# Half-chunk weight buffers, and two weight sums of the value products added on chip

## The chip, the cores and the metric

The kernel runs on one core of a Trainium2 chip. The metric is the device time of one execution, in microseconds (us). Before the change the median of three runs is 1919.06 us (1919.06 to 1919.16).

The engines go by the names of the profile: PE does matmuls (PEld is its weight load), DVE is VectorE, ACT is ScalarE, POOL is GpSimd, and SP only issues DMA transfers. Each engine runs its own instructions strictly in order, and waits for the others by semaphores.

## The reference

Two layers, each with one wide input projection, three groups of attention heads, a gate, an output projection and a layer norm:

```python
def hybrid_layer(x, mem, w_in, b_forget, w_mem_kv, w_out, ln_gain, ln_bias):
    ...
    h = jnp.einsum('bsd,dn->bsn', x, w_in)
    ...
    y_fox = fox_attention(heads(fq, H_FOX), heads(fk, H_FOX), heads(fv, H_FOX), cum_logf)
    y_fox = y_fox.reshape(b, s, D_FOX) * jax.nn.silu(fg)
    ...
    y_dsa = dsa_attention(...)
    y_mem = memory_attention(heads(mq, H_MEM), k_mem..., v_mem...)
    y = jnp.concatenate([y_fox, y_dsa, y_mem], axis=-1)
    y = jnp.einsum('bsn,nd->bsd', y, w_out)
    return layer_norm(ALPHA * x + y, ln_gain, ln_bias)
```

The sequence has 512 rows, the model 2048 columns, and everything is float32. The change touches only one piece of `x @ w_in`: the columns that make the heads' values, their gates and the first queries and keys, called "values" here.

## The kernel before, in words

**Chunks and halves.** All weights come as chunks of 128x2048 float32 (1 MB), in one long list that sets the order of the program (the main loop at L1051). `load_w` (L234) has SP load a chunk into one of three buffers `raw` (8 KB per partition). A chunk is used in two halves of 1024 columns. `split_w` (L256) splits a half into a high and a low part: ACT writes `whi` (L213), DVE writes `wlo = raw - whi` (L214), into a pool of four pairs. PE then does three matmuls per product, whi by the high part of the left side (L220), wlo by the same (L221), whi by its low part (L222). A half of a value chunk is 12 such matmuls of 512 columns, a chunk 24.

**The order around the change.** Nothing is scheduled by a planner: the main loop writes each engine's instructions in program order. When it stands at half n of chunk i, it first issues `grow_w(i)` and `load_w(i + 2)`, then `split_w(n + 3)`, then PE's matmuls of half n. Between these, `tick` steps generators that make everything else: sums of x for the left sides (`val_operands`, vx, vxh and vxl), the search for the top keys, the stores of values, and `all_sums`.

**Seven products in place of eight.** The value matrix is multiplied as 2x2 blocks with seven products per pair of columns, four pairs to a layer. A product is named (P1, P7, P2, Q6, Q4, Q5, Q3), and each uses either a plain block of weights or a sum of blocks: P7 uses T3 (two blocks), Q6 uses T2, Q4 uses T4, Q5 uses T1 (two blocks). Each has two chunks, g0 and g1. A layer first does P1 P1 P7 P7 P2 Q6 Q6 P2 Q4 Q4 for the four pairs (`VAL_FIRST`), and then Q5 Q5 Q3 Q3 for the four pairs (`VAL_SECOND`), 56 chunks in all. Results are gathered by DVE in `vraw` and added up in DRAM by accumulating stores of POOL.

**Where the sums come from.** T3 and T1 are summed in DRAM by POOL (`weight_sums`, L360): a copy of one block (L377), then an accumulating transfer of the other (L358). Outside the values stage each step is preceded by a tiny `mark` of DVE and `seen` of POOL (`pool_waits`), which hold POOL's queue to DVE's place in the program. SP loads the finished sum like a chunk. T2 and T4 are grown in place: once P7's raw chunk has been split, `grow_w` (L245) has POOL add one block to it in SBUF by an accumulating transfer, which gives Q6's chunk, and one more gives Q4's.

**The next x.** At the end of the first layer `next_x` (L933) normalises 16 tiles z and transposes them into 16 pairs of high and low parts, the odd low parts on POOL (L950), and then stores the 16 tiles to DRAM from POOL's queue (L956).

Of the kernel before, what the change touches and what calls it, by code (L numbers as in the profile page):

```python
# [11 lines left out]
F32 = mybir.dt.float32  # L12
# [74 lines left out]
VAL_OPENS = ("P1", "P7", "P2", "Q5")  # L87
VAL_ENDS = ("P1", "Q4", "P2", "Q3")
GROWN = {"Q6": ("P7", (0, 0)), "Q4": ("Q6", (1, 0))}


def layer_chunks(l):
# [27 lines left out]
def stream():  # L120

    wall = all_chunks()
    where = {c: i for i, c in enumerate(wall)}
    out = []

    def product(kind, l, name, pair, gs=(0, 1)):
        right = PRODUCTS[name][2]
        for g in gs:
            if kind == "val" and name in GROWN:
                of, step = GROWN[name]  # L130
                src = ("grown", (of, where[kind, l, 2 * pair + step[1], 2 * step[0] + g]))
            elif isinstance(right, str):
                src = ("sum", (kind, l, right, pair, g))
            else:
                src = ("wall", where[kind, l, 2 * pair + right[1], 2 * right[0] + g])
            out.append(({"val": "vs"}.get(kind, kind), l, (name, pair), g, src))

    for i, c in enumerate(wall):
        kind, l, j = c[:3]
        if kind == "out":  # L140
            if c == ("out", l, 0, 0):
                for name, pair in OUT_ORDER:
                    product("out", l, name, pair)
        elif kind == "val":
            if c == ("val", l, 0, 0):
                for order in (VAL_FIRST, VAL_SECOND):
                    for pair in range(PAIRS):
# [25 lines left out]
def kernel(  # L173
# [12 lines left out]
):  # L186
    nc = tc.nc
    consts = ctx.enter_context(tc.tile_pool(name="consts", bufs=1))
    raws = ctx.enter_context(tc.tile_pool(name="raws", bufs=3))
    whl = ctx.enter_context(tc.tile_pool(name="whl", bufs=4))  # L190
    slots = ctx.enter_context(tc.tile_pool(name="slots", bufs=71))
    tiny = ctx.enter_context(tc.tile_pool(name="tiny", bufs=3))
# [6 lines left out]
    def uid(name):  # L199
        count[0] += 1  # L200
        return f"{name}_{count[0]}"
# [23 lines left out]
    chunks = stream()  # L225
    raw, parts = {}, {}
    sums = {}
    grows = {}
    place = {c[:4]: i for i, c in enumerate(chunks)}
    for i, (kind, l, j, g, (how, key)) in enumerate(chunks):  # L230
        if how == "grown":
            grows[place[kind, l, (key[0], j[1]), g]] = i

    def load_w(i, pieces=1):  # L234
        if i < len(chunks) and chunks[i][4][0] != "grown":
            raw[i] = raws.tile([P, DM], F32, tag="raw", name=uid("raw"))
            w = DM // pieces
            kind, key = chunks[i][4]
            src = wall[key] if kind == "wall" else sums[key]
            for c in range(pieces):  # L240
                nc.sync.dma_start(raw[i][:, c * w:(c + 1) * w], src[:, c * w:(c + 1) * w])
                if i < 3 and c * 2 % pieces == 0:
                    load_mem(2 * i + c * 2 // pieces)

    def grow_w(i):  # L245

        if i in grows:
            n = grows[i]
            nc.gpsimd.dma_start(raw[n], wall[chunks[n][4][1][1]], accum_op=ALU.add,
                                max_dma_last_dim=4 * DM)  # L250

    def last_half(i):

# [2 lines left out]
    def split_w(n, pieces=1, between=None):  # L256
        i, h = divmod(n, 2)
        if i < len(chunks):
            if last_half(i) and n < 2 * len(chunks) - 3:
                parts[n] = []  # L260
                for c in range(2):
                    hi, lo = slot("wh", F32R), slot("wl", F32R)
                    split(raw[i][:, h * 1024 + c * 512:h * 1024 + (c + 1) * 512], hi, lo)
                    parts[n].append((hi, lo))
                return
            hi = whl.tile([P, DM // 2], F32R, tag="whi", name=uid("whi"))
            lo = whl.tile([P, DM // 2], F32R, tag="wlo", name=uid("wlo"))
            w = DM // 2 // pieces
            for c in range(pieces):
                r = slice(c * w, (c + 1) * w)  # L270
                split(raw[i][:, h * 1024 + c * w:h * 1024 + (c + 1) * w], hi[:, r], lo[:, r])
                if between and c == 0:
                    between()
            parts[n] = (hi, lo)
            if last_half(i):
                parts[n] = [(hi[:, c:c + 512], lo[:, c:c + 512]) for c in (0, 512)]
            if h:
                t = raw.pop(i)
                if i in grows:
                    raw[grows[i]] = t  # L280


    mem_raw = {}

# [104 lines left out]
    def all_sums():  # L389


        for l in range(DEPTH):
            yield from paced(weight_sums("val", l, ("T3", "T1"), range(PAIRS)))
            while now != (l, "heads"):
                yield 1
            yield from paced(weight_sums("out", l, ("T3", "T1", "T2", "T4"), range(2)))
# [382 lines left out]
    def val_operands():  # L779
        add, sub = ALU.add, ALU.subtract  # L780
        a11, a12, a21, a22 = (0, 0), (0, 1), (1, 0), (1, 1)

        for i in range(4):
            val_sum("S3", i, ((a11, 0, add), (a21, 0, sub), (a11, 1, add), (a21, 1, sub)))
            yield 1
        for i in range(4):
            val_hi("S3", i)
            val_sum("S2", i, (("S3", 0, add), (a22, 0, add), (a22, 1, add)))
            yield 1
            val_lo("S3", i)  # L790
            yield 1
        for i in range(4):
            hi, lo = vleft["S2", i] = slot("vxh", F32R), slot("vxl", F32R)
            nc.scalar.activation(hi, vx["S2", i], AF.Copy, scale=-1.0)
            yield 1
            nc.vector.scalar_tensor_tensor(lo, vx["S2", i], -1.0, hi.bitcast(F32),
                                           op0=ALU.mult, op1=ALU.subtract)
        yield from wait_for("P7")
        making.append("S1")
        for n in range(9):  # L800
            if n < 4:
                val_sum("S1", n, ((a11, 0, add), ("S2", 0, sub), (a11, 1, add)))
# [12 lines left out]
        making.clear()  # L815
# [116 lines left out]

    def next_x():  # L933

        ms = [norm_stats(st) for st in range(4)]
        for c in range(4):
            for st in range(4):
                normalise(st, c, *ms[st])
            yield 1
        for k in range(KT):  # L940
            c, o = divmod(k, 4)
            tp = bank("xt")
            for st in range(4):
                nc.tensor.transpose(tp[:, st * P:(st + 1) * P], z[st, c][:, o * P:(o + 1) * P], ident)
            xf, hi, lo = slot("xf"), slot("xh", F32R), slot("xl", F32R)
            nc.scalar.activation(xf, tp, AF.Identity, bias=gcol[:, 1, k:k + 1],
                                 scale=gcol[:, 0, k:k + 1])
            nc.scalar.activation(hi, xf, AF.Copy)
            eng = nc.gpsimd if k % 2 else nc.vector
            eng.tensor_tensor(lo, xf, hi.bitcast(F32), op=ALU.subtract)  # L950
            xT[k] = (hi, lo)
            if k % 2:
                yield 1
        for c in range(4):
            for st in range(4):
                nc.gpsimd.dma_start(x1_d[st * P:(st + 1) * P, c * 512:(c + 1) * 512], z.pop((st, c)))  # L956
                if st % 2:
                    yield 1

    def residual_rows(l):  # L960

# [89 lines left out]
    for i, (kind, l, j, col, _) in enumerate(chunks):  # L1051
# [27 lines left out]
            ps = bank("c")  # L1079
        for h in range(2):  # L1080
            n = 2 * i + h
            if h == 0 and i > 0:
                grow_w(i)
                load_w(i + 2)
                if 2 <= i < 6:
                    for k in range(4 * i - 8, 4 * i - 4):
                        load_xt(k)
                elif i == 7:
                    load_tables()
            if n < 6:  # L1090
                split_mem(n + 2)
            split_w(n + 3)
# [267 lines left out]
```

## Time and profile before

| what | us |
|---|---|
| median of three runs | 1919.06 |
| the profiled execution | 1918.99 |
| its span in the profile | 1916.8 |
| PE busy | 1900.9 |
| DVE busy | 1389.3 |
| ACT busy | 969.6 |
| POOL busy | 355.8 |

The profile shows one execution. Times in it count from the start of the span. A row of a group or of a timeline reads: line, engine, operation, output<-input, shape; behind it are the busy time and what ended the idle time before it. A row of waits reads: who waited for whom, us in total, times, the longest. The values of layer 0 run from 249 to 557 us (the pairs of Q5 and Q3 from 469), those of layer 1 from 1200 to 1508 (Q5 and Q3 from 1420).

### The profile page before, as it was taken

To read this page: it belongs to the slowest core of one execution; us is meant where nothing else is said; L and a number is where in the kernel's file an instruction comes from. 1 tells how busy PE (TensorE), PEld (TensorE's weight loads), DVE (VectorE), ACT (ScalarE), POOL (GpSimd) and SP (SyncE) were. 2 spreads that over 40 slices of the span, in tenths; PEclk is the share of its full clock that TensorE was granted. 3 is DMA by queue.
4 is the path that set the end of the run, shared out by engine and by line. 5 is a ranking of instruction groups with operands and counts; after the bars stand their busy time and mean duration, and the time that the engine had idled before them with its cause. 6 is when DMAs were issued, how large, how long until landed. Compare 5 with 4: busy or idle time off the path is not lost.

```text
span 1916.8 us, 25327 instructions
## 1 busy us (share of the span) xinstructions
PE 1900.9 (99%) x9282; PEld 1620.7 (85%) x9282; DVE 1389.3 (72%) x2343; ACT 969.6 (51%) x1538; POOL 355.8 (19%) x615
## 2 busy tenths in 40 slices
PE   9999999999999999999999999999999999999997
PEld 8998888888888888888899988888888888888886
DVE  6666657779665677688776777667786666677898
ACT  5565454445444455555475644544454444555552
POOL 0231101111123012110052212111111321112101
PEclk9999999999999999999999999999999999999999
DMA  9699888888988778898778989988889888789856
GB/s 365 230 296 323 213 194 235 241 234 239 263 257 233 245 236 240 250 333 310 247 234 269 283 272 258 238 220 236 244 244 261 261 227 244 240 234 268 342 197 154
DMA packets 110712, 484.57 MB, mean 253 GB/s; under 512 B 11504, under 2 KB 44272, under 8 KB 69500
## 3 DMA queue, kind: packets, MB, share of 16 engines
q0 software_dynamic: 32864, 216.05, 45.6%
q1 hardware_dynamic: 77724, 266.90, 38.8%
q8 instruction: 73, 1.20, 0.3%
q14 instruction: 51, 0.42, 0.1%
HBM read 445.14 MB, written 174.09 MB: 323 GB/s over the span
## 4 chain that ended last, share of the span: by engine, by line
PE 93%; DVE 4%; ACT 2%; issue 1%; DMA 0%; SPq 0%; POOL 0%; DVEq 0%; ACTq 0%; POOLq 0%
PE c L220 12%; PE c L222 12%; PE c L221 12%; PE v L222 11%; PE v L220 11%; PE v L221 11%; PE z L221 4%; PE z L222 4%; PE z L220 4%; PE pt L682 1%; PE ix L600 1%; PE ix L599 1%; PE po L222 1%; PE po L221 1%; PE po L220 1%
## 5 line engine op out<-in xcount | busy, mean ns | idle before, releaser
L214 DVE TENSOR_TENSOR wlo<-raw,whi 128x1024 fp32r<-128x1024 f32 (+1 forms) x497 | 607.0, 1225 | 283.5 <-ACT whi L213 281.3
L213 ACT ACTIVATE whi<-raw 128x1024 fp32r<-128x1024 f32 (+1 forms) x497 | 521.9, 1054 | 381.5 <-PE v L222 243.1
L220 PE MATMUL c<-xh,whi 128*128 128x512 f32 (+1 forms) x1056 | 402.1, 381 | 0.0
L222 PE MATMUL c<-xh,wlo 128*128 128x512 f32 (+1 forms) x1056 | 398.3, 377 | 0.0
L221 PE MATMUL c<-xl,whi 128*128 128x512 f32 (+1 forms) x1056 | 397.3, 376 | 0.0
L222 PEld LDWEIGHTS c<-xh,wlo 128*128 128x128 f32 x1056 | 198.2, 188 | 32.4
L221 PEld LDWEIGHTS c<-xl,whi 128*128 128x128 f32 x1056 | 198.5, 188 | 30.5
L220 PEld LDWEIGHTS c<-xh,whi 128*128 128x128 f32 x1056 | 198.3, 188 | 30.0
L220 PE MATMUL v<-whi,vxh 128*128 128x512 f32 x512 | 199.8, 390 | 0.0
L222 PE MATMUL v<-whi,vxl 128*128 128x512 f32 x512 | 199.3, 389 | 0.0
L221 PE MATMUL v<-wlo,vxh 128*128 128x512 f32 x512 | 199.2, 389 | 0.0
L349 POOL TENSOR_TENSOR seen<-mark,mhalf 128x1 f32<-128x1 f32 x128 | 35.3, 276 | 762.2 <-DVE mark L348 727.3
L221 PE MATMUL z<-wlo,yh 128*128 128x512 f32 (+1 forms) x434 | 168.1, 387 | 2.5 <-DVE wlo L214 2.5
L220 PE MATMUL z<-whi,yh 128*128 128x512 f32 (+1 forms) x434 | 168.4, 388 | 0.0
L222 PE MATMUL z<-whi,yl 128*128 128x512 f32 (+1 forms) x434 | 167.8, 387 | 0.0
L220 PE MATMUL v<-whi,xh 128*128 128x512 f32 x384 | 149.4, 389 | 0.0
L221 PE MATMUL v<-wlo,xh 128*128 128x512 f32 x384 | 149.4, 389 | 0.0
L222 PE MATMUL v<-whi,xl 128*128 128x512 f32 x384 | 149.4, 389 | 0.0
L222 PEld LDWEIGHTS v<-whi,vxl 128*128 128x128 f32 x512 | 96.1, 188 | 20.0
L221 PEld LDWEIGHTS v<-wlo,vxh 128*128 128x128 f32 x512 | 96.1, 188 | 19.9
L220 PEld LDWEIGHTS v<-whi,vxh 128*128 128x128 f32 x512 | 96.1, 188 | 19.6
L221 PEld LDWEIGHTS z<-wlo,yh 128*128 128x128 f32 x434 | 81.5, 188 | 20.0 <-DVE wlo L214 4.2
(220 smaller groups left out, 3031.0 us busy)
## 6 DMA issues: line engine op xcount, KB each, us to landing
raw<-in_wall_dram SPq DMA_DIRECT2D x151, 1024.0 KB, 7.2
sum<-in_wall_dram POOLq DMA_DIRECT2D x64, 1024.0 KB, 11.5
raw<-sum SPq DMA_DIRECT2D x64, 1024.0 KB, 7.1
raw<-in_wall_dram POOLq DMA_DIRECT2D x32, 1024.0 KB, 8.1
v<-vraw POOLq DMA_DIRECT2D x96, 256.0 KB, 4.2
vraw<-v SPq DMA_DIRECT2D x64, 256.0 KB, 6.9
x<-z POOLq DMA_DIRECT2D x32, 256.0 KB, 8.1
memraw<-in_memt_dram SPq DMA_DIRECT2D x16, 256.0 KB, 7.3
```

The costliest lines, as they stand in the source:

```text
L213: nc.scalar.activation(hi, src, AF.Copy)
L214: nc.vector.tensor_tensor(lo, src, hi.bitcast(F32), op=ALU.subtract)
L220: nc.tensor.matmul(ps, ah, bh, start=start, stop=False, skip_group_check=more)
L221: nc.tensor.matmul(ps, ah, bl, start=False, stop=False, skip_group_check=more)
L222: nc.tensor.matmul(ps, al, bh, start=False, stop=stop, skip_group_check=more)
L349: nc.gpsimd.tensor_tensor(seen, mark, mhalf, op=ALU.mult)
L599: nc.tensor.matmul(o, st[:, qb * P:(qb + 1) * P], kh2[:, :w], start=True, stop=False)
L600: nc.tensor.matmul(o, st[:, qb * P:(qb + 1) * P], kl2[:, :w], start=False, stop=True)
L682: nc.tensor.transpose(tp[tb][:, toff + (qb - kt) * P:toff + (qb - kt + 1) * P], pr[b][:, off + kt * P:off + (kt + 1) * P], ident)
```

## The change

**Buffers.** `raw` becomes six buffers of half a chunk in place of three of a whole one, in the same space. A chunk is loaded in two transfers of 512 KB, and each half comes free by itself.

**T4 on DVE.** Q4's sum is no longer grown by a transfer. T4 is T2 plus a block, and that block is the one that P2 has just used. `make_w` adds P2's raw half to Q6's in place, behind the split of whichever comes later in the program. T2 is still grown by POOL, by halves.

**T1 on DVE.** The chunk of Q5 is no longer loaded as a finished sum. SP loads one block into the raw half and the other into two small slots `other` (128x512), and `pair_w(n + 4)` adds them, one half earlier than `split_w(n + 3)`. `weight_sums` for the values makes T3 alone.

**Two smaller edits.** `val_operands` waits six steps before the splits of S2 (`yield 6`), and `next_x` stores column c - 1 while it makes column c.

```diff
-    raws = ctx.enter_context(tc.tile_pool(name="raws", bufs=3))
+    raws = ctx.enter_context(tc.tile_pool(name="raws", bufs=6))
...
+            elif kind == "val" and right in PAIRED:
+                src = ("pair", tuple(at(step) for step in PAIRED[right]))
...
+            if j[0] == "Q6":
+                grows[of] = i
+            else:
+                lender = place[kind, l, ("P2", j[1]), g]
+                makes[max(of, lender)] = i
+                lends[i] = (of, lender)
...
+                if c * 2 % pieces == 0:
+                    raw[i].append(raws.tile([P, H], F32, tag="raw", name=uid("raw")))
+                nc.sync.dma_start(raw[i][-1][:, c * w % H:c * w % H + w], src[:, c * w:(c + 1) * w])
...
+                if kind == "pair":
+                    for e in (2 * c, 2 * c + 1):
+                        t = slot("other")
+                        nc.sync.dma_start(t, wall[key[1]][:, e * 512:(e + 1) * 512])
+                        others[i, e] = t
...
+    def pair_w(n):
+
+        i, h = divmod(n, 2)
+        if i < len(chunks) and chunks[i][4][0] == "pair":
+            for e in range(2):
+                d = raw[i][h][:, e * 512:(e + 1) * 512]
+                nc.vector.tensor_tensor(d, d, others.pop((i, 2 * h + e)), op=ALU.add)
...
+    def make_w(i, h):
+
+        to = makes[i]
+        of, lender = lends[to]
+        t = raw.setdefault(to, [None, None])[h] = raw[of][h]
+        nc.vector.tensor_tensor(t, t, raw[lender][h], op=ALU.add)
+        raw[of][h] = raw[lender][h] = None
...
+            if i in makes:
+                make_w(i, h)
...
-            yield from paced(weight_sums("val", l, ("T3", "T1"), range(PAIRS)))
+            yield from paced(weight_sums("val", l, ("T3",), range(PAIRS)))
...
+        yield 6
         for i in range(4):
             hi, lo = vleft["S2", i] = slot("vxh", F32R), slot("vxl", F32R)
...
+                for st in (o - 1, o) if c else ():
+                    store(st, c - 1)
                 yield 1
...
+            grow_w(n + 2)
             if h == 0 and i > 0:
-                grow_w(i)
                 load_w(i + 2)
...
+            pair_w(n + 4)
             if n < 6:
                 split_mem(n + 2)
             split_w(n + 3)
```

How this moves instructions is shown at three places of layer 0. The first is DVE's order where the first Q5 chunks are prepared. In the kernel before, the halves of pair 0's two Q5 chunks give the wlo rows numbered 4253, 4275, 4295 and 4321. Here is the piece from the second to the last of these:

```order
L214 TENSOR_TENSOR wlo_4275<-raw_4228,whi_4274 128x1024
L777 TENSOR_TENSOR vxl_4250<-vx_2310,vxh_4249 128x512
L214 TENSOR_TENSOR wlo_4295<-raw_4272,whi_4294 128x1024
L859 TENSOR_TENSOR vraw_3954<-vraw_3954,v_3961 128x512
L859 TENSOR_TENSOR vraw_3956<-vraw_3956,v_3962 128x512
L767 TENSOR_TENSOR vx_2531<-xh_678,vx_2531 128x256
L767 TENSOR_TENSOR vx_2531<-vx_2531,xl_679 128x256
L767 TENSOR_TENSOR vx_2531<-xh_682,vx_2531 128x256
L767 TENSOR_TENSOR vx_2531<-vx_2531,xl_683 128x256
L214 TENSOR_TENSOR wlo_4321<-raw_4272,whi_4320 128x1024
```

In the changed kernel the same four halves are the wlo rows 4290, 4324, 4346 and 4374 (L218). L275 is `pair_w`. What is left out are the sums of x, the vxl and two adds of results, as before:

```order
L275 TENSOR_TENSOR raw_4251<-raw_4251,other_4253 128x512
L275 TENSOR_TENSOR raw_4251<-raw_4251,other_4255 128x512
...
L275 TENSOR_TENSOR raw_4257<-raw_4257,other_4259 128x512
L275 TENSOR_TENSOR raw_4257<-raw_4257,other_4261 128x512
L218 TENSOR_TENSOR wlo_4290<-raw_4251,whi_4289 128x1024
...
L275 TENSOR_TENSOR raw_4309<-raw_4309,other_4311 128x512
L275 TENSOR_TENSOR raw_4309<-raw_4309,other_4313 128x512
L218 TENSOR_TENSOR wlo_4324<-raw_4257,whi_4323 128x1024
...
L275 TENSOR_TENSOR raw_4315<-raw_4315,other_4317 128x512
L275 TENSOR_TENSOR raw_4315<-raw_4315,other_4319 128x512
L218 TENSOR_TENSOR wlo_4346<-raw_4309,whi_4345 128x1024
...
L218 TENSOR_TENSOR wlo_4374<-raw_4315,whi_4373 128x1024
```

Eight adds of 128x512 stand ahead of the last of the four, two for each half. Each pair of adds comes one half before the wlo that reads it.

The second place is DVE's order a little earlier, at the last P2 and Q6 chunks. Before:

```order
L214 TENSOR_TENSOR wlo_4092<-raw_3920,whi_4091 128x1024
L777 TENSOR_TENSOR vxl_4065<-vx_4041,vxh_4064 128x512
L214 TENSOR_TENSOR wlo_4112<-raw_4089,whi_4111 128x1024
...
L214 TENSOR_TENSOR wlo_4134<-raw_4089,whi_4133 128x1024
L777 TENSOR_TENSOR vxl_4109<-vx_4083,vxh_4108 128x512
L214 TENSOR_TENSOR wlo_4154<-raw_3881,whi_4153 128x1024
```

and in the changed kernel, where L293 is `make_w`:

```order
L218 TENSOR_TENSOR wlo_4114<-raw_3936,whi_4113 128x1024
L823 TENSOR_TENSOR vxl_4086<-vx_4061,vxh_4085 128x512
L218 TENSOR_TENSOR wlo_4134<-raw_4109,whi_4133 128x1024
L293 TENSOR_TENSOR raw_3934<-raw_3934,raw_4109 128x1024
...
L218 TENSOR_TENSOR wlo_4156<-raw_4111,whi_4155 128x1024
L293 TENSOR_TENSOR raw_3936<-raw_3936,raw_4111 128x1024
L823 TENSOR_TENSOR vxl_4131<-vx_4104,vxh_4130 128x512
L218 TENSOR_TENSOR wlo_4177<-raw_3892,whi_4176 128x1024
```

Two adds of 128x1024 have come in here, behind the wlo of the two halves of P2's g1. Two more stand behind the halves of Q6's g0, four and three wlo rows earlier than the first of these. All four stand ahead of the rows of the first place.

The third place is SP's queue. Before, a chunk is one row, and pair 0's Q5 chunks are loaded from the finished sums:

```order
L241 DMA raw_3964<-in_wall_dram 128x2048
L241 DMA raw_4089<-in_wall_dram 128x2048
L241 DMA raw_4228<-sum_1605 128x2048
L241 DMA raw_4272<-sum_1660 128x2048
L241 DMA raw_4318<-in_wall_dram 128x2048
```

In the changed kernel the same chunk of P2 and the first of Q5:

```order
L258 DMA raw_4109<-in_wall_dram 128x1024
L258 DMA raw_4111<-in_wall_dram 128x1024
L258 DMA raw_4251<-in_wall_dram 128x1024
L264 DMA other_4253<-in_wall_dram 128x512
L264 DMA other_4255<-in_wall_dram 128x512
L258 DMA raw_4257<-in_wall_dram 128x1024
L264 DMA other_4259<-in_wall_dram 128x512
L264 DMA other_4261<-in_wall_dram 128x512
```

A Q5 chunk is six transfers in place of one, and twice the bytes. PE's order is the same in both kernels; POOL loses 16 copies, 16 accumulating steps and the marks of these (T1, over both layers), and 16 transfers that grew Q4.

More of the change, by code (lines that the diff above doesn't have):

```diff
@@ L89 @@
 GROWN = {"Q6": ("P7", (0, 0)), "Q4": ("Q6", (1, 0))}
+PAIRED = {"T1": ((0, 0), (0, 1))}
 def layer_chunks(l):
@@ L128, in product @@
         for g in gs:
+            at = lambda step: where[kind, l, 2 * pair + step[1], 2 * step[0] + g]
             if kind == "val" and name in GROWN:
                 of, step = GROWN[name]
-                src = ("grown", (of, where[kind, l, 2 * pair + step[1], 2 * step[0] + g]))
+                src = ("grown", (of, at(step)))
+            elif kind == "val" and right in PAIRED:
+                src = ("pair", tuple(at(step) for step in PAIRED[right]))
             elif isinstance(right, str):
@@ L134, in product @@
             else:
-                src = ("wall", where[kind, l, 2 * pair + right[1], 2 * right[0] + g])
+                src = ("wall", at(right))
             out.append(({"val": "vs"}.get(kind, kind), l, (name, pair), g, src))
@@ L227 @@
     sums = {}
-    grows = {}
+    grows, makes, lends = {}, {}, {}
     place = {c[:4]: i for i, c in enumerate(chunks)}
@@ L231, with half, load_w @@
         if how == "grown":
-            grows[place[kind, l, (key[0], j[1]), g]] = i
-    def load_w(i, pieces=1):
+            of = place[kind, l, (key[0], j[1]), g]
+            if j[0] == "Q6":
[4 more added lines that the diff above has]
+                lends[i] = (of, lender)
+    H = DM // 2
+    def half(src, h):
+        return src[:, h * H:(h + 1) * H]
+    def load_w(i, pieces=2):
@@ L235, in load_w @@
         if i < len(chunks) and chunks[i][4][0] != "grown":
-            raw[i] = raws.tile([P, DM], F32, tag="raw", name=uid("raw"))
-            w = DM // pieces
             kind, key = chunks[i][4]
-            src = wall[key] if kind == "wall" else sums[key]
+            src = {"wall": lambda: wall[key], "sum": lambda: sums[key],
+                   "pair": lambda: wall[key[0]]}[kind]()
+            raw[i], w = [], DM // pieces
             for c in range(pieces):
-                nc.sync.dma_start(raw[i][:, c * w:(c + 1) * w], src[:, c * w:(c + 1) * w])
+                if c * 2 % pieces == 0:
+                    raw[i].append(raws.tile([P, H], F32, tag="raw", name=uid("raw")))
+                nc.sync.dma_start(raw[i][-1][:, c * w % H:c * w % H + w], src[:, c * w:(c + 1) * w])
@@ L242, in load_w @@
                 if i < 3 and c * 2 % pieces == 0:
                     load_mem(2 * i + c * 2 // pieces)
-    def grow_w(i):
+                if kind == "pair":
[3 more added lines that the diff above has]
+                        others[i, e] = t
+    others = {}
+    def pair_w(n):
[4 more added lines that the diff above has]
+                nc.vector.tensor_tensor(d, d, others.pop((i, 2 * h + e)), op=ALU.add)
@@ L247, in grow_w @@
+    def grow_w(n):
+        i, h = divmod(n, 2)
         if i in grows:
-            n = grows[i]
-            nc.gpsimd.dma_start(raw[n], wall[chunks[n][4][1][1]], accum_op=ALU.add,
+            to = grows[i]
+            t = raw.setdefault(to, [None, None])[h] = raw[i][h]
+            nc.gpsimd.dma_start(t, half(wall[chunks[to][4][1][1]], h), accum_op=ALU.add,
                                 max_dma_last_dim=4 * DM)
+            if h:
+                del raw[i]
+    def make_w(i, h):
[4 more added lines that the diff above has]
+        raw[of][h] = raw[lender][h] = None
@@ L258, in split_w @@
         if i < len(chunks):
+            r = raw[i][h]
             if last_half(i) and n < 2 * len(chunks) - 3:
@@ L262, in split_w @@
                     hi, lo = slot("wh", F32R), slot("wl", F32R)
-                    split(raw[i][:, h * 1024 + c * 512:h * 1024 + (c + 1) * 512], hi, lo)
+                    split(r[:, c * 512:(c + 1) * 512], hi, lo)
                     parts[n].append((hi, lo))
[L265 to L280, printed above, removed]
+            else:
+                hi = whl.tile([P, H], F32R, tag="whi", name=uid("whi"))
+                lo = whl.tile([P, H], F32R, tag="wlo", name=uid("wlo"))
+                w = H // pieces
+                for c in range(pieces):
+                    q = slice(c * w, (c + 1) * w)
+                    split(r[:, q], hi[:, q], lo[:, q])
+                    if between and c == 0:
+                        between()
+                parts[n] = (hi, lo)
+                if last_half(i):
+                    parts[n] = [(hi[:, c:c + 512], lo[:, c:c + 512]) for c in (0, 512)]
+            if i in makes:
+                make_w(i, h)
+            elif i not in grows and i not in held:
+                raw[i][h] = None
+    held = {i for pair in lends.values() for i in pair}
     mem_raw = {}
@@ L933, in next_x, with store @@
     def next_x():
+        def store(st, c):
+            nc.gpsimd.dma_start(x1_d[st * P:(st + 1) * P, c * 512:(c + 1) * 512], z.pop((st, c)))
         ms = [norm_stats(st) for st in range(4)]
@@ L952, in next_x @@
             if k % 2:
+                for st in (o - 1, o) if c else ():
+                    store(st, c - 1)
                 yield 1
[L954 to L958, printed above, removed]
+        for st in range(4):
+            store(st, 3)
+            if st % 2:
+                yield 1
     def residual_rows(l):
```

## The prediction

> **What bounds the kernel now.** I read the page's busy shares and its chain first, because they say which engine a new microsecond must land on to be seen, and then PE's waits.
>
> ```profile
> span 1916.8 us, 25327 instructions
> PE 1900.9 (99%) x9282; PEld 1620.7 (85%) x9282; DVE 1389.3 (72%) x2343; ACT 969.6 (51%) x1538; POOL 355.8 (19%) x615
> PE 93%; DVE 4%; ACT 2%; issue 1%; DMA 0%; SPq 0%; POOL 0%; DVEq 0%; ACTq 0%; POOLq 0%
> ...
> PE z L221 <- DVE wlo L214: 2.5, 4, 0.7
> PE warm L319 <- POOL mhalf L321: 1.4, 1, 1.4
> PE v L220 <- ACT memh L213: 0.6, 1, 0.6
> PE v L221 <- DVE wlo L214: 0.2, 1, 0.2
> PE v L220 <- ACT whi L213: 0.2, 1, 0.2
> ```
>
> TensorE is busy for 1900.9 of 1916.8 us and does the same matmuls in the same order after the change. Its waits add up to 4.9 us (2.5 + 1.4 + 0.6 + 0.2 + 0.2). That is the most that any change to transfers or to VectorE can win here, and a loss has no such limit. None of the five is a DMA wait: four matmuls of the output projection (tile z) wait for a weight's low part, and the rest lies in the lead-in. So the change can hardly help, and the question is what it does to the stretch it touches, the value products of each layer, where PE does not wait at all.
>
> The table by stage shows that stretch: first the end of the Q4 products, then the four column pairs of Q5 and Q3, and at the end the same two places in layer 1. The columns are PE, PEld, DVE, ACT and POOL busy, the granted clock, the DMA share and GB/s.
>
> ```profile
> 425.00:447.00 22.00, 22.00 (x98) 18.21 (x98) 16.74 (x27) 11.22 (x13) 2.62 (x3) 1.00 0.85 182
> 447.00:469.00 22.00, 22.00 (x98) 18.21 (x97) 20.77 (x35) 10.58 (x12) 3.30 (x6) 1.00 0.85 267
> 469.00:491.00 22.00, 22.00 (x99) 18.20 (x97) 16.69 (x23) 11.25 (x14) 3.36 (x5) 1.00 0.83 266
> 491.00:513.00 22.00, 22.00 (x99) 18.22 (x98) 14.41 (x22) 10.90 (x13) 3.67 (x5) 1.00 0.97 271
> 513.00:535.00 22.00, 22.00 (x99) 18.22 (x98) 15.71 (x23) 10.90 (x14) 3.59 (x5) 1.00 0.89 257
> 535.00:557.00 22.00, 22.00 (x102) 18.21 (x101) 16.21 (x21) 11.13 (x14) 8.71 (x12) 1.00 0.94 258
> ...
> 1398.00:1420.00 22.00, 22.00 (x99) 18.21 (x98) 20.78 (x35) 10.57 (x12) 3.61 (x7) 1.00 0.87 269
> 1420.00:1442.00 22.00, 22.00 (x99) 18.22 (x98) 16.68 (x23) 11.22 (x13) 3.16 (x5) 1.00 0.83 263
> ```
>
> PE is full and the clock is whole everywhere. VectorE, at 72% over the span, is at 20.77 of 22 us from 447 to 469, just where the first Q5 chunks are prepared, and layer 1 has the same peak (20.78). The average over the span hides this.
>
> **What the change moves.** POOL loses 32 transfers of weight sums in DRAM and 16 that grew a chunk; VectorE gets 32 adds of 128x1024 (T4, `make_w`) and 64 of 128x512 (T1, `pair_w`), half of them in each layer. Most T4 adds fall where VectorE waits for ACT in any case, and cost nothing there. The order lists show which do not: in the last pair's tail, four T4 adds and then the eight T1 adds of pair 0 all stand ahead of one instruction, the low part (wlo) of the last half of pair 0's Q5. I call it the key half. The VectorE timeline of the kernel before gives prices and room:
>
> ```profile
> 434.94 1.23 DVE L214 TENSOR_TENSOR wlo<-raw,whi 128x1024 fp32r<-128x1024 f32 x1 [1.49 <-ACT whi L213]
> ...
> 438.80 1.22 DVE L214 TENSOR_TENSOR wlo<-raw,whi 128x1024 fp32r<-128x1024 f32 x1
> 440.53 1.23 DVE L214 TENSOR_TENSOR wlo<-raw,whi 128x1024 fp32r<-128x1024 f32 x1 [0.51 <-ACT whi L213]
> ...
> 445.87 1.23 DVE L214 TENSOR_TENSOR wlo<-raw,whi 128x1024 fp32r<-128x1024 f32 x1 [0.79 <-ACT whi L213]
> ...
> 448.60 1.22 DVE L214 TENSOR_TENSOR wlo<-raw,whi 128x1024 fp32r<-128x1024 f32 x1
> ...
> 451.31 1.22 DVE L214 TENSOR_TENSOR wlo<-raw,whi 128x1024 fp32r<-128x1024 f32 x1 [0.88 <-ACT whi L213]
> ...
> 453.17 0.69 DVE L854 TENSOR_TENSOR vraw<-vraw,vraw 128x512 f32<-128x512 f32 x1
> 453.78 0.68 DVE L852 SCALAR_TENSOR_TENSOR vraw<-v,vraw 128x512 f32<-128x512 f32 x1
> ...
> 456.70 1.22 DVE L214 TENSOR_TENSOR wlo<-raw,whi 128x1024 fp32r<-128x1024 f32 x1
> 457.83 0.68 DVE L777 TENSOR_TENSOR vxl<-vx,vxh 128x512 fp32r<-128x512 f32 x1
> ...
> 472.48 1.22 DVE L214 TENSOR_TENSOR wlo<-raw,whi 128x1024 fp32r<-128x1024 f32 x1
> ...
> 481.67 1.23 DVE L214 TENSOR_TENSOR wlo<-raw,whi 128x1024 fp32r<-128x1024 f32 x1 [1.78 <-ACT whi L213]
> ```
>
> *Prices.* Two instructions overlap a little, so a backlog grows by start-to-start time. A 128x1024 add from two SBUF tiles like the wlo at 456.70 holds the engine until 457.83, 1.13 us; a 128x512 like the one at 453.17 until 453.78, 0.61 us. Four T4 adds cost 4 x 1.13 = 4.52 us, eight T1 adds 8 x 0.61 = 4.88 us, together 9.40 us.
>
> [...]
>
> *Room.* The last four T4 adds follow the wlo of 434.94, 438.80, 445.87 and 448.60. Behind the first of them VectorE idles three times before it is busy without a break: 0.51, 0.79 and 0.88 us. Each idle is counted from the modelled end of the instruction before, 0.09 us after the next could have started (1.22 - 1.13), so the room is 2.18 + 0.27 = 2.45 us. From 451.31 to the idle of 1.78 us before 481.67 there is none. The key wlo therefore moves by 9.40 - 2.45 = 6.95 us.
>
> *Lead.* It now starts at 472.48 and ends at 473.70; PE reads it first with the L221 matmul:
>
> ```profile
> 477.17 0.39 PE L220 MATMUL v<-whi,vxh 128*128 128x512 f32 x1
> 477.40 0.39 PE L221 MATMUL v<-wlo,vxh 128*128 128x512 f32 x1
> ...
> 1423.68 1.22 DVE L214 TENSOR_TENSOR wlo<-raw,whi 128x1024 fp32r<-128x1024 f32 x1
> ...
> 1428.61 0.39 PE L221 MATMUL v<-wlo,vxh 128*128 128x512 f32 x1
> ```
>
> The lead is 477.40 - 473.70 = 3.70 us, in layer 1 1428.61 - 1424.90 = 3.71 us. PE then waits 6.95 - 3.70 = 3.25 us in each layer, 6.5 us in both. It will come in pieces: the halves just before have leads only slightly larger, so PE should wait a little at several wlo of Q5 pair 0, 3.25 us in sum. While PE waits, ACT's and VectorE's work for later halves catches up. The following pairs have eight T1 adds (4.88 us) per 22 us, and 22 - 16.69, 22 - 14.41 and 22 - 15.71 us of room, so they hold.
>
> *Bounds of it.* With whole durations it is 1 us more per layer. Downward, what could be smaller is the backlog. The 1.49 us before 434.94 counts only if the first T4 adds stood ahead of it, and the order list says they do not; if one did, the wait would be 1.13 us less. So 2.1 to 4.3 us per layer.
>
> *Transfers.* DRAM traffic falls by the vanished sums, but in Q5 itself it rises: eight chunks per layer load 2 MB in place of 1.
>
> ```profile
> DMA packets 1097, 5.84 MB, mean 266 GB/s; under 512 B 129, under 2 KB 129, under 8 KB 513
> ...
> q1 hardware_dynamic: 647, 4.77, 62.5%
> q0 software_dynamic: 448, 1.05, 20.2%
> ...
> DMA packets 3340, 9.53 MB, mean 381 GB/s; under 512 B 375, under 2 KB 375, under 8 KB 2950
> ...
> raw<-in_wall_dram SPq DMA_DIRECT2D x151, 1024.0 KB, 7.2
> ```
>
> The first three rows are from 469 to 491; the fourth, from 5 to 30, is what full queues reach, 381 GB/s. The four Q5/Q3 windows (266, 271, 257, 258) average 263 GB/s. Eight times 1.05 MB in 88 us are 95 GB/s more, 358 in all: 94% of 381, so by bytes it fits, and the price is 0. By shares it does not. The windows average 0.91 (POOL's accumulating stores take 20.2% for 1.05 MB, SP's loads 62.5% for 4.77), and 8.4 MB at 381 GB/s is 22 us of all engines against 0.09 x 88 = 8 us free, a lag of 14 us at the end of Q3. Three chunks of buffer come round in 3 x 5.44 = 16.3 us (24 matmuls of 0.227 us each), a load lands in 7.2, and `pair_w` asks for it one half (2.72 us) earlier, so 6.4 us of lag are free, and the wait for VectorE gives 3.25 more: at worst 14 - 6.4 - 3.25 = 4.3 us per layer. I take 0, because a share of 0.97 from 491 to 513 went by without any wait of PE, and both ends stay in the range.
>
> [...]
>
> *The rest costs nothing.* POOL's part of the next x is a row of `xl` subtractions with idle before each, where two stores of 0.54 us (12 took 6.48) fit; without it each odd k would cost 1.1 us on POOL:
>
> ```profile
> 985.93 1.29 POOL L950 TENSOR_TENSOR xl<-xf,xh 128x512 fp32r<-128x512 f32 x1 [2.21 <-ACT xh L948]
> ...
> 994.84 6.48 POOL L956 DMA_DIRECT2D x<-z  x12
> ```
>
> `yield 6` moves four splits of S2 behind other work that PE needs sooner. The half loads of SP are more instructions on a queue that nothing waits for. The removed marks are 128x1 writes. No term for any of these.
>
> **Sum.** Against the profiled execution's 1918.99 us (span 1916.8 and 2.2 around it): + 6.5 + 0 = 1925.5 us. The median of the runs, 1919.06, is 0.07 higher, nothing beside this.
>
> **Rivals.**
> *A, the loads of Q5 become the bound.* The share (0.91 on average, 0.97 at the peak) speaks for it, the bytes against. Place: raw or `other` landing late in pairs 2 and 3; price up to 4.3 us per layer on top, 1934 us; with half the lag beyond the cover, 1930.
> *B, it is hidden: not slower.* If the twelve adds meet enough idle, the key wlo slips less than its 3.70 us and PE never waits: 1919 us. That needs 3.25 us more room than the rows show. For it: 16.74 of 22 us busy from 425 to 447 leaves 5.3 us idle before the peak, and if ACT's whi came earlier with half buffers VectorE could work ahead into it. Against: whi mostly waits for PE to free one of four weight buffers, which the change leaves at four (243.1 of its 381.5 us idle):
>
> ```profile
> L213 ACT ACTIVATE whi<-raw 128x1024 fp32r<-128x1024 f32 (+1 forms) x497 | 521.9, 1054 | 381.5 <-PE v L222 243.1
> ```
> At a backlog 1.3 us smaller in each layer it would already count as the same.
> *C, faster: the low parts of the output stage come earlier.* Mechanism: raw buffers that come free by halves start loads earlier, ACT's whi follows, and the four z waits go: 2.5 us, 1916.5; with all of the lead-in's waits gone too, 1914.1. Against: the rows name VectorE, and nothing of its work in that stage is removed.
>
> That the change does not do what it says has no share: the adds stand in the program's order.
>
> **Numbers.** Forecast (wait of 2 to 4.3 us per layer at Q5 pair 0) 0.56, A 0.17, B 0.22, C 0.05. A measurement here tells 0.2% (3.8 us) from no change, so below 1915.2 is faster and above 1922.9 slower. The forecast's own range is 1923.2 to 1927.6. Forecast and A are slower, together 0.73, of which I give 0.01 to the edge: slower 0.72. B and most of C, which ends at 1916.5, are the same: 0.25. Faster needs nearly all 4.9 us of PE's waits: 0.03. The range reaches into B and over most of A: 1919 to 1932.
>
> **What would show it.** Right: PE waits "v L221 <- DVE wlo" of about 3 us in sum shortly after 470 and shortly after 1421, VectorE near 22 of 22 us from 447 to 480, and no PE wait elsewhere in the values. A shows as idle before `raw<-raw,other` that a DMA ends, in pairs 2 and 3, with the DMA share at 1.00. B shows as wlo of the key half ending before PE's L221 with both traces' PE cadence equal. C shows as a PE waits list without the four z rows. Wrong would be: PE waiting in the values before 460, where I count the T4 adds at nothing, or at layer 1's first chunks near 1004, where I count the stores at nothing.

## The result, and the profile after

The changed kernel takes 1935.97 us (median of four runs, 1935.27 to 1937.01), against 1919.06 before: a ratio of 1.0089 with an interval of 1.0071 to 1.0106. It is slower by 16.9 us. The forecast was slower by 6.5 us, 1925.5, with a range that ended at 1932. The profiled execution of the changed kernel took 1935.78 us, 16.8 more than the one before. Of all executions below, one of the ten with T4 alone took 4955.86 us in the slow state; without it the median there is 1922.2 in place of 1922.51.

The page of the kernel after, with the rows that answer to those shown of before:

```profile
span 1933.6 us, 26103 instructions
PE 1907.8 (99%) x9282; PEld 1621.9 (84%) x9282; DVE 1462.4 (76%) x2407; ACT 970.4 (50%) x1538; POOL 323.5 (17%) x551
PE 87%; DVE 8%; ACT 2%; issue 1%; DMA 0%; SPq 0%; POOL 0%; DVEq 0%; ACTq 0%; POOLq 0%
```

and PE's waits in the kernel after (who waited for whom, us in total, times, the longest):

```profile
PE v L224 <- ACT vraw L910: 5.3, 2, 2.6
PE v L225 <- DVE wlo L218: 5.1, 8, 0.9
PE z L225 <- DVE wlo L218: 2.5, 4, 0.7
PE warm L365 <- POOL mhalf L367: 1.4, 1, 1.4
PE v L224 <- ACT whi L217: 0.5, 1, 0.5
```

Two things stand here. The late wlo now make PE idle for 5.1 us in eight pieces; six of them, 4.7 us, lie in the values, three in each layer, and the other two in the lead-in. Those six are the wait of the forecast. Above it stands a wait that the forecast does not have: two matmuls of 2.6 us each that waited for ACT's `vraw` (L910, the copies of a finished product out of PSUM). And PE's busy time has risen by 6.9 us with the same matmuls, so some of them became slower.

The table by stage shows where (PE, PEld, DVE, ACT and POOL busy, the clock granted to PE as a share of its full speed, DMA share, GB/s). The first four rows are the windows shown of before, the others the place itself in smaller steps:

```profile
447.00:469.00 22.00, 21.41 (x95) 17.42 (x94) 21.72 (x35) 8.43 (x10) 3.30 (x6) 1.00 0.80 264
469.00:491.00 22.00, 17.60 (x66) 12.92 (x65) 21.80 (x35) 9.83 (x12) 2.90 (x4) 0.92 0.81 274
491.00:513.00 22.00, 22.00 (x98) 18.21 (x97) 16.71 (x25) 10.66 (x12) 3.42 (x4) 1.00 1.04 329
513.00:535.00 22.00, 22.00 (x98) 18.20 (x97) 19.57 (x30) 10.66 (x12) 3.44 (x4) 1.00 1.06 348
...
484.00:487.00 3.00, 0.41 (x2) 0.00 (x0) 2.97 (x6) 2.08 (x4) 0.00 (x0) 1.00 0.99 330
487.00:491.00 4.00, 3.97 (x10) 3.18 (x11) 4.00 (x6) 1.41 (x2) 1.82 (x2) 0.57 1.01 380
491.00:495.00 4.00, 4.00 (x19) 3.30 (x18) 3.09 (x5) 1.61 (x2) 0.00 (x0) 1.00 1.07 274
```

VectorE is full (21.72 and 21.80 of 22 us) where 20.77 and 16.69 stood before. PE does 66 matmuls from 469 to 491 in place of 99. From 484 to 487 it stands still, and from 487 to 491 it does 10 matmuls in 4 us at a granted clock of 0.57, where 17 or 18 would fit. After that nothing is lost: pairs 1 to 3 run at full pace, though the DMA share there is 1.03 to 1.06.

The chain of waits of the kernel after, taken from 480 to 492, tells in order how the standstill came about (start, us, what):

```profile
483.66 0.77 DVE vx L813 x2
484.43 0.02 issue
484.46 0.44 DVE vx L813
484.89 0.02 issue
484.92 0.04 ACT vxh L818
...
485.45 1.04 ACT whi L217
486.49 0.49 ACT vraw L910
486.98 0.04 issue
487.03 0.80 PE v L224
487.82 0.43 PE v L225
488.25 0.43 PE v L226
```

VectorE finishes a sum of x (`vx`) that Q3 reads only in its last half. ACT, in order, stands at the split of this sum (`vxh`), and behind it come one `whi` and then the two copies of Q5 pair 0's result. Q3 accumulates into the very banks (pieces of PSUM, in which PE adds up a product) that these copies read, so PE cannot begin Q3 before them: its first matmul there, at 487.03, waited 2.62 us. Here are the same instructions in the kernel before, the end of the sum on VectorE and then ACT, where all of this was early enough:

```profile
476.59 0.42 DVE L767 TENSOR_TENSOR vx<-vx,xl 128x256 f32<-128x256 f32 x1
...
477.05 0.63 ACT L772 ACTIVATE vxh<-vx 128x512 fp32r<-128x512 f32 x1 [1.28 <-DVE vx L767]
477.59 1.05 ACT L213 ACTIVATE whi<-raw 128x1024 fp32r<-128x1024 f32 x1
478.73 0.60 ACT L863 ACTIVATE vraw<-v 128x512 f32<-128x512 f32 x1
480.09 0.60 ACT L863 ACTIVATE vraw<-v 128x512 f32<-128x512 f32 x1 [0.76 <-PE v L222]
```

Already before, `vxh` waited for VectorE (1.28 us). The sum ended at 477.01 (476.59 + 0.42), the first copy at 479.33, and PE was ready for Q3 at 479.9 (477.17 and one half of 2.72): a slack of about 0.6 us, against a lead of 3.70 for the wlo that I had priced. In the changed kernel the sum ends at 484.88, 7.87 us later, and the key wlo starts 7.86 us later.

These rows of the kernel after show the first and the last of the wlo pieces in layer 0, with the key wlo between them:

```profile
467.88 0.50 PE L225 MATMUL v<-wlo,xh 128*128 128x512 f32 x1 [0.59 <-DVE wlo L218]
...
480.34 1.22 DVE L218 TENSOR_TENSOR wlo<-raw,whi 128x1024 fp32r<-128x1024 f32 x1
...
481.61 0.50 PE L225 MATMUL v<-wlo,vxh 128*128 128x512 f32 x1 [0.87 <-DVE wlo L218]
```

The first piece, about 0.85 us with the restart, falls in the last half of Q4 (its left side is a part of x itself, `xh`), ahead of Q5; layer 1 has one there too. By the restart I mean that the matmuls next to a wait start some 0.33 us apart in place of 0.227.

In sum, from the starts of successive matmuls less the 0.227 us that one takes: in layer 0 3.6 us at the wlo, 2.8 us at the copies and 1.7 us of slow matmuls, 8.05 in all; in layer 1 3.4, 2.8 and 1.5, 7.7. Together 15.8 of the 16.8 us between the two profiled executions; of the rest some 0.6 us lie in the lead-in, the others in small pieces.

### The profile page after: what moved, and what is told of

Its sections match the earlier page's. It is cut to its first block, busy times and chain, and to the rows that moved or that the text cites. A ratio compares the mean times of both kernels' runs of the same rounds, so it can differ in the third digit from the quotient of the medians.

```text
span 1933.6 us, 26103 instructions
## 1 busy us (share of the span) xinstructions
PE 1907.8 (99%) x9282; PEld 1621.9 (84%) x9282; DVE 1462.4 (76%) x2407; ACT 970.4 (50%) x1538; POOL 323.5 (17%) x551
## 4 chain that ended last, share of the span: by engine, by line
PE 87%; DVE 8%; ACT 2%; issue 1%; DMA 0%; SPq 0%; POOL 0%; DVEq 0%; ACTq 0%; POOLq 0%
PE c L224 12%; PE c L226 12%; PE c L225 12%; PE v L224 10%; PE v L226 10%; PE v L225 10%; PE z L225 4%; PE z L226 4%; PE z L224 4%; DVE wlo L218 3%; PE pt L728 1%; DVE vx L813 1%; PE ix L646 1%; PE ix L645 1%; PE po L226 1%
## 5 line engine op out<-in xcount | busy, mean ns | idle before, releaser
L218 DVE TENSOR_TENSOR wlo<-raw,whi 128x1024 fp32r<-128x1024 f32 (+1 forms) x497 | 606.7, 1225 | 217.9 <-ACT whi L217 215.8
L395 POOL TENSOR_TENSOR seen<-mark,mhalf 128x1 f32<-128x1 f32 x96 | 25.9, 270 | 618.5 <-DVE mark L394 614.5
```

The lines of the kernel that those rows point to most:

```text
L218: nc.vector.tensor_tensor(lo, src, hi.bitcast(F32), op=ALU.subtract)
L395: nc.gpsimd.tensor_tensor(seen, mark, mhalf, op=ALU.mult)
```

## The experiments

The theory (V) was now this: all of the loss is VectorE's backlog, which reaches PE by two ways, at once through wlo and, one product later, through ACT's queue; and the longer of the two waits makes PE's clock fall. Its rivals: W, only the late wlo cost; D, the doubled loads of Q5 cost (rival A of the prediction); C, the clock falls for some other reason.

### T4 alone on VectorE

```diff
-PAIRED = {"T1": ((0, 0), (0, 1))}
+PAIRED = {}
...
-            yield from paced(weight_sums("val", l, ("T3",), range(PAIRS)))
+            yield from paced(weight_sums("val", l, ("T3", "T1"), range(PAIRS)))
```

> The changed kernel with T1 of the values summed in DRAM again (Q5 loaded as finished sums); T4 stays on VectorE, half buffers and the small edits stay. Theory V (VectorE's backlog, passed on to ACT's queue and from there to PE): the backlog at Q5 pair 0 is four T4 adds less the room, 4.52 - 2.45 = 2.07 us, below the lead of 3.70 us, so no wlo wait. The sum of x that ACT's last vxh waits for ends at 477.01 in the kernel before, and in the changed one PE starts Q3 2.15 us after it (484.88 to 487.03). 477.01 + 2.07 + 2.15 = 481.23 against 479.9, where PE is ready: a wait of about 1.3 us per layer, too short for the clock to fall (waits of 1.0 us were not followed by slow matmuls), 1921 to 1922 us. Theory D (the doubled loads of Q5): without them all of the loss is gone, 1919 us. Theory W (only late wlo, as predicted): 1919 us.

Measured: 1922.51 us, ratio 1.0018 (1.0009 to 1.0028). The trace of this run has no wlo wait of note, and the wait for the copies in both layers. Its PE rows at this place:

```profile
482.05 0.50 PE L224 MATMUL v<-whi,vxh 128*128 128x512 f32 x1 [1.49 <-ACT vraw L910]
482.39 0.40 PE L225 MATMUL v<-wlo,vxh 128*128 128x512 f32 x1
482.62 0.39 PE L226 MATMUL v<-whi,vxl 128*128 128x512 f32 x1
```

With the restart this is 1.65 us (1.3 expected), and the matmuls behind it follow at the full pace of 0.23 us. Both D and W expected nothing here. So the smaller backlog is hidden from wlo and reaches PE through ACT alone: that way has almost no slack.

### T1 alone on VectorE

```diff
-            if j[0] == "Q6":
+            if j[0] in ("Q6", "Q4"):
                 grows[of] = i
```

> The changed kernel with Q4's T4 grown by POOL's transfers again, by halves; T1 stays on VectorE. Theory V: the backlog at Q5 pair 0 is eight T1 adds, 4.88 us. wlo waits 4.88 - 3.70 = 1.2 us plus some 0.2 for restarts; the vraw copies make PE wait as long as in the changed kernel, 477.01 + 4.88 + 2.15 = 484.04 against 479.9 + 1.4 = 481.3, 2.7 us, and the clock falls after it as there (1.9 us): 5.8 us per layer, 1930 to 1931 us. Theory D: the loads are all there, 1936 us. Theory W: 1.2 us per layer, 1921.5 us.

Measured: 1929.1 us, ratio 1.0053 (1.0038 to 1.0068). In the trace the starts give 2.79 us at the copies in each layer, and slow matmuls behind both; the wlo waits (2.4 us idle) are down to one of about a microsecond per layer and small ones. V's price was 1 to 2 us too high. It counted the slow matmuls in every execution, and they do not seem to be in every one: the profiled one, 1931.03 us, has a mean clock of 0.996, the two at 1928.1 have 0.998, as the kernel before. D, which needed all of the loss, and W are out. The two parts of the change do not add up either: 3.3 us for the one alone and 9.9 for the other, 16.9 together. The wait at wlo has a threshold, the lead: the 2.07 us of the T4 adds alone stay below it, and behind the T1 adds they come on top (4.7 us of idle in the values with both, 1.8 with T1 alone). The slow matmuls that are not in every execution would make up the other part.

### One split on ACT moved behind the copies

```diff
+            if n == 7:
+                yield 1
             if n < 8:
                 val_hi(*(("S1", n), ("S4", n - 4))[n > 3])
```

> The changed kernel in which one instruction stands later: the last split of S4 (one vxh of 128x512 on ACT) comes behind ACT's two copies of Q5 pair 0's result instead of in front of them. No add and no load changes. Theory V: the copies no longer wait for VectorE's sum of x, so the wait of 2.8 us and the slow matmuls behind it (1.9 us) go in both layers, and the late wlo stay: 1936.0 - 9.4 = 1926 to 1927 us. Theory D: no load changes, so nothing does, 1936 us. Theory C (the clock falls by itself or because of the wlo waits): the wait of 2.8 us goes and the slow matmuls stay, 1930 us.

Measured: 1928.02 us, ratio 1.0047 (1.0032 to 1.0062). Moving one instruction on ACT, and with it the `vxl` of the same sum on VectorE, which comes one half later too, wins 8 us of the 16.9. The wait at Q3 of pair 0 and the slow matmuls are gone; its PE waits are:

```profile
PE v L225 <- DVE wlo L218: 4.9, 7, 0.9
PE z L225 <- DVE wlo L218: 2.5, 4, 0.7
PE v L224 <- ACT vraw L912: 1.6, 1, 1.6
```

V forecast 1926 to 1927. The microsecond over it is seen in the third row: in layer 1's third pair the copies stand behind a `whi` whose raw half landed late (1.54 us). So D has a part after all; in the changed kernel it does not show, probably because the longer waits in front cover it.

### The adds without the second loads

```diff
-                        t = slot("other")
-                        nc.sync.dma_start(t, wall[key[1]][:, e * 512:(e + 1) * 512])
-                        others[i, e] = t
+                        others[i, e] = raw[i][-1][:, (1 - e % 2) * 512:(2 - e % 2) * 512]
```

> The changed kernel without the 64 loads of the second block of T1: pair_w adds the two 512-column quarters of the half itself instead (so Q5's second block is left out of the result). VectorE has the same 96 adds of the same shapes; SP loads 1 MB per Q5 chunk as before the change. Theory V: all the loss stays, 1935 to 1936 us. Theory D: all of it goes, 1919 to 1921 us; if both carry a part, between.

Measured: 1935.66 us, ratio 1.0088 (1.0071 to 1.0105): all of the loss stays when the loads go. The DMA traffic from 491 to 557 falls from 332 to 261 GB/s. D as the cause of the 16.9 us is out. A small part of it is not: each half's second add here reads what the first has just written and takes a little longer, some 0.5 us per layer (see the next section), and the wlo waits are 5.6 us in place of 5.1.

This run shows something on the clock too. In layer 0 its wait at Q3 was the same, and the matmuls behind it were not slow:

```profile
487.16 0.50 PE L224 MATMUL v<-whi,vxh 128*128 128x512 f32 x1 [2.58 <-ACT vraw L908]
487.50 0.39 PE L225 MATMUL v<-wlo,vxh 128*128 128x512 f32 x1
487.73 0.40 PE L226 MATMUL v<-whi,vxl 128*128 128x512 f32 x1
```

and the window behind it in the same kernel:

```profile
487.00:491.00 4.00, 3.84 (x17) 3.19 (x18) 3.96 (x6) 2.28 (x4) 1.82 (x2) 1.00 0.62 169
```

The clock stayed at 1.00 (17 matmuls in the 4 us in which the changed kernel did 10). In layer 1 of the same execution it fell. So a wait of 2.8 us from start to start sometimes costs 1.5 to 1.7 us more and sometimes not. A reading of what decides it stands in the last section.

### Late split, without the second loads

> The run with the late split (1928.0 us), without the 64 loads of T1's second block; the adds take the other quarter of the half (Q5's second block is left out of the result). Theory V with D behind it: the wait of 1.7 us in layer 1's third pair, where ACT's copies stood behind a raw half that landed late, goes; the late wlo stay, 3.6 us per layer: 1926 us. If that wait has nothing to do with the loads: 1928 us.

Measured: 1928.37 us, ratio 1.005 (1.0033 to 1.0067), where 1926 was expected. The wait in layer 1's third pair is gone, as D's part says, but the time is not better than with the loads. The replacement was not a clean one: each half's second add now reads what the first has just written, and two of them take 1.33 us to the next instruction (465.03 to 466.36) in place of 1.21 with a separate tile (463.67 to 464.88). That makes 0.5 us more backlog over the four halves, and the late wlo cost 5.3 us in place of 4.9 as idle. The size of D's part is therefore not settled by this run.

### Both sums undone

> The changed kernel with both sums undone: T1 in DRAM and Q4's T4 grown by POOL (by halves), no add on VectorE. What is left of the change are the six half buffers, the loads in two transfers, the six steps in front of the splits of S2 and the earlier stores of the next x. Theory V: no backlog, so no wait in the values and 1919 us within 1. A theory that the half buffers or the small edits cost something of themselves: 1920 us or more.

Both edits of the first two experiments together. Measured: 1919.05 us, ratio 1.0001 (0.9991 to 1.001). The half buffers, the loads in two transfers, the six steps and the earlier stores neither cost nor bring anything, as I had priced them.

### T4 on VectorE, with the late split

> T1 in DRAM, T4 on VectorE (as in the run with T4 alone, 1922.5 us), and the last split of S4 on ACT behind the copies of Q5 pair 0's result. Theory V: the backlog of 2.07 us is below wlo's lead of 3.70, and ACT's copies no longer wait for it, so both waits of 1.65 us go: 1919 us within 1. If the backlog reaches PE by another way as well: 1920 to 1922 us.

Measured: 1919.16 us, ratio 1.0001 (0.9991 to 1.001). The 3.3 us of T4 alone were the copies' wait and nothing else; with it out of the way the 32 adds of 128x1024 on VectorE cost nothing that shows.

### T1 of the later pairs alone, with T4 and the late split

```diff
-            elif kind == "val" and right in PAIRED:
+            elif kind == "val" and right in PAIRED and pair:
...
             yield from paced(weight_sums("val", l, ("T3",), range(PAIRS)))
+            yield from paced(weight_sums("val", l, ("T1",), range(1)))
```

> T1 of pair 0 summed in DRAM again, T1 of pairs 1 to 3 added on VectorE (48 adds, 48 loads of a second block), T4 on VectorE, and the late split. Theory V: the adds cost only where they stand on VectorE's peak; ahead of the key half there are the four T4 adds, 2.07 us, which the lead covers, and the later pairs have room: 1919 to 1920 us. Theory D: the DMA share of 1.04 to 1.07 in pairs 1 to 3 costs PE something by itself: 1921 to 1923 us, with waits behind raw or other.

Measured: 1920.2 us, ratio 1.0007 (0.9998 to 1.0017), runs from 1918.3 to 1923.3. So 80 of the 96 adds cost nothing on VectorE once the 16 on the peak are taken away (eight in each layer). What is left is D, and in the profiled execution (1921.87 us) it can be seen. ACT's timeline there, in pair 2:

```profile
519.13 1.06 ACT L217 ACTIVATE whi<-raw 128x1024 fp32r<-128x1024 f32 x1 [4.00 <-DMA raw<-in_wall_dram]
521.64 1.06 ACT L217 ACTIVATE whi<-raw 128x1024 fp32r<-128x1024 f32 x1 [1.45 <-DMA raw<-in_wall_dram]
524.26 1.06 ACT L217 ACTIVATE whi<-raw 128x1024 fp32r<-128x1024 f32 x1 [1.56 <-DMA raw<-in_wall_dram]
525.22 1.07 ACT L913 ACTIVATE vraw<-v 128x512 f32<-128x512 f32 x2
...
525.86 0.50 PE L224 MATMUL v<-whi,vxh 128*128 128x512 f32 x1 [1.97 <-ACT vraw L913]
```

and the window around it:

```profile
513.00:535.00 22.00, 20.04 (x89) 16.24 (x88) 17.22 (x26) 9.12 (x11) 3.60 (x4) 1.00 1.05 343
```

Three raw halves in a row land late, at a DMA share of 1.05 and 343 GB/s, ACT stands at their `whi`, and the copies behind them make PE wait for 2 us: the same queue as above, with a transfer in VectorE's place. Over the ten runs the loss is about 1 us on the median and up to 4; one of the ten was profiled, so that it has this cause in the others is not shown.

### T1 alone, with the late split

> The run with T1 alone on VectorE (1929.1 us), with the late split. Theory V: the bank wait of 2.79 us and the slow matmuls behind it go, the wlo waits stay (1.8 us per layer there): 1919.1 + 3.6 = 1922 to 1924 us, the upper end with one wait for a late load. If the eight adds reach PE by another way as well: 1925 us or more.

Measured: 1924.98 us, ratio 1.0032 (1.002 to 1.0045), a microsecond above what V expected, and at the border of "another way" (1925). Its trace, of an execution of 1926.91 us, has 2.7 us of wlo waits and 2.2 us for copies. These last are, as above, in the third pairs (2.0 and 0.3 us). No other wait shows in the values, so "another way" has no sign in the trace. Against T1 alone the late split wins 4 us.

### The T1 adds on POOL, with the late split

```diff
-            nc.vector.tensor_tensor(d, d, others.pop((i, 2 * h + e)), op=ALU.add)
+            nc.gpsimd.tensor_tensor(d, d, others.pop((i, 2 * h + e)), op=ALU.add)
```

> The changed kernel with the 64 T1 adds on POOL in place of VectorE, and the late split. Theory V: VectorE has only the T4 adds ahead of the key half, 2.07 us, which its lead covers. POOL has per pair eight adds of 1.3 to 1.9 us (its xl of the same shape: 1.29 alone, 1.9 on the mean) and four stores of 0.9, 14 to 19 of 22 us, so it keeps up: 1919 to 1921 us, with one wait of 1.7 us for a late load perhaps. Rival P (POOL does not keep up or slows VectorE): PE waits for whi behind raw from POOL, over 1924 us.

Measured: 1963.15 us, ratio 1.0232 (1.0216 to 1.0247), the slowest of all, where 1919 to 1921 was expected. Rival P is right, in its second half: POOL was not the one that fell behind, as its 64 adds have a mean of 1735 ns, within what was assumed. VectorE was held up, and PE waited 28.5 us for wlo. The timelines of POOL and VectorE in this run:

```profile
466.39 7.38 POOL L275 TENSOR_TENSOR raw<-raw,other 128x512 f32<-128x512 f32 x6
...
466.06 8.01 DVE L813 TENSOR_TENSOR vx<-xh,vx 128x256 f32<-128x256 f32 x1
474.10 0.42 DVE L813 TENSOR_TENSOR vx<-vx,xl 128x256 f32<-128x256 f32 x1
```

The group of wlo from 469 to 557 in this kernel (count, busy us, mean ns, idle before):

```profile
L218 DVE TENSOR_TENSOR wlo<-raw,whi 128x1024 fp32r<-128x1024 f32 x26 | 55.5, 2149 | 8.8 <-ACT whi L217 8.7
```

and in the kernel before the change:

```profile
L214 DVE TENSOR_TENSOR wlo<-raw,whi 128x1024 fp32r<-128x1024 f32 x33 | 40.8, 1236 | 23.4 <-ACT whi L213 23.1
```

One add of 128x256, 0.42 us elsewhere, took 8.01 us while POOL did six adds. The mean wlo went from 1236 to 2149 ns. In this kernel, work of this kind cannot be given to POOL to relieve VectorE. No version that was run beats the kernel before; three come out the same as it.

## Why the prediction was wrong

- *What bounds it*: right. PE has no wait in the values before, POOL's and the transfers' relief brought nothing (both sums undone: 1919.05; T4 with the late split: 1919.16).
- *The place*: right. The loss is at Q5 pair 0 and the start of Q3 in both layers, behind VectorE's peak of 20.77 of 22 us; only the first piece of about 0.8 us comes one half earlier than forecast, at the end of Q4. Without the T1 adds of pair 0, and with the late split, nearly all of it is gone (1920.2).
- *The wlo term*, 3.25 us per layer "in pieces": right in mechanism and nearly in size. The starts give 3.6 and 3.4 us. The key wlo began at 480.34, where 472.48 + 6.95 = 479.43 was forecast, and PE's first use of it came at 481.61, after 0.87 us of the last of several waits. Each piece costs 0.1 to 0.2 us more than its idle, for the restart.
- *The step that failed*: "While PE waits, ACT's and VectorE's work for later halves catches up." I priced the backlog at the one reader with a lead of 3.70 us and did not follow it to VectorE's other readers. `vx` is late by the same amount, ACT's `vxh` waits for it, and behind `vxh` in ACT's queue stand the copies that set PE's banks free, with some 0.6 us of slack. The row of ACT that waits 1.28 us for `vx` was in the trace of before. This missing term is 2.8 us per layer, and 1.6 us more for the clock that falls after it: 4.4 of the 8 us per layer. T4 alone (1.65 us per layer by this way and none by wlo) and the late split (8 us won) show this way by itself.
- *The slow matmuls*: no step had them. I took the granted clock of 1.00 as given, because in the kernel before PE never stands still for long; here 2.6 us of idle in one piece were followed by a fall in both layers (last section).
- *Transfers*: 0 was taken and up to 4.3 us per layer allowed. In the changed kernel itself the doubled loads show no wait of PE. Where VectorE's waits are gone they come out, about 1 us on the median and up to 4 in a run, in pair 2 at a share of 1.05, one of the two places that rival A named, but small. The share was the better guide than the bytes: raw halves landed late at some 340 GB/s (the mean over 22 us in pair 2, with T1 of the later pairs), below the 381 of full queues.
- *Rivals B and C*: out. The adds were not hidden, and the four waits of the output stage are there unchanged (2.5 us).
- *The range* ended at 1932 because it held the forecast and rival A but no second way from VectorE to PE.

## What to carry to other kernels

When work is added to an engine that is full for a while, list every reader of that engine's results, and behind each reader the instructions queued in order after it; the slack that counts is the smallest over all of them, not that of the reader nearest to the bound. Here a late operand (`vx`) blocked an unrelated eviction (the copies), and the eviction held a bank: PE waited 2.6 us for it in each layer. Issuing the eviction ahead of work that nobody needs yet lifted the block: this was worth 8 us, and cost nothing that shows.

## What the runs showed of the hardware

**The clock.** After some waits of PE, matmuls started every 0.427 us in place of 0.227, at a granted clock of one half, for 3.41 us. The waits of 2.8 us from start to start (2.6 us idle) had this in both layers of the changed kernel and of T1 alone, and in one layer of two without the second loads. The single waits of 1.65 to 2.13 us in the other runs with VectorE's adds did not: behind 1.49 us of idle with T4 alone (482.05) and 1.97 us with T1 of the later pairs (525.86) the matmuls followed every 0.23 us. In the trace of the changed kernel the falls stand on a grid: from the fall at 487.03 to the next, at 1446.17, are 959.14 us, or 281 steps of 3.413, and from there to the last, at 1927.45, 481.28 us, or 141 steps. Here are the two steps around the fall in layer 0 of the changed kernel, and two of the same length in which the wait without the second loads lies that was spared:

```profile
483.62:487.03 3.41, 0.79 (x5) 0.33 (x3) 3.34 (x7) 2.12 (x4) 0.00 (x0) 1.00 1.00 341
487.03:490.44 3.41, 3.41 (x8) 2.74 (x9) 3.41 (x5) 1.38 (x2) 1.82 (x2) 0.50 0.99 376
...
482.70:486.11 3.41, 1.88 (x9) 1.17 (x7) 3.34 (x7) 1.47 (x3) 0.00 (x0) 1.00 0.76 223
486.11:489.53 3.42, 2.37 (x10) 1.99 (x11) 3.38 (x6) 2.44 (x4) 1.82 (x2) 1.00 0.69 216
```

The first wait has 2.62 us of idle in one step (3.41 - 0.79), and the next step ran at half clock. The second, cut at 486.11, has 1.53 us in one step and 1.05 in the next, and the clock stayed. The traces of the kernel before and of the changed one, cut into such steps at their falls, agree: of PE's idle as the profile counts it, each step at full clock with 2.24 us or more was followed by one at half clock, none with 1.27 or less was. That it matters where a wait lies on the grid is my reading of these rows; no run placed a wait there on purpose. So in these runs the single waits of up to 2.13 us cost only themselves, and those of 2.8 us either nothing beyond that or 1.5 to 1.7 us more.

**VectorE and POOL.** While POOL added two SBUF tiles, VectorE's adds and subtractions of two SBUF tiles were held up: one took 8.01 us in place of 0.42, and from 469 to 557 the mean wlo took 2149 ns in place of 1236 and the mean `vxl` 1117 in place of 684. Not all were: the adds of `xl` to `vx` had a mean of 425 ns there against 424 before.
